# First modulation by halves of the channels, with the first four projection units begun on the first half

## Chip, core and metric

The kernel runs on one core of one Trainium2 chip. The metric is the device time of one execution in microseconds, lower is better. The time before is the median of three runs, 2643.65 us (2641.43 to 2645.2).

## What is computed

One layer of a hybrid diffusion backbone over 1024 latent tokens and 256 context tokens of 1024 channels. What bears on the change is its beginning:

```python
mod = (jax.nn.silu(c) @ w_mod[l] + b_mod[l])[:, None, :]
sh1, sc1, g1, sh2, sc2, g2 = jnp.split(mod, 6, axis=-1)
modc = (jax.nn.silu(c_ctx) @ w_mod[l] + b_mod[l])[None, None, :]
...
xn = modulate(rms_norm(x), sh1, sc1)
cn = modulate(rms_norm(h_ctx), csh1, csc1)
yg, xr, q, k, v, gr, gn = split_in(xn @ w_in[l] + b_in[l])
```

Behind it come the recurrent branch, neighbourhood attention, the merge and a mixture of 16 experts, which the change leaves alone.

## The kernel before

All weights come as chunks of 128 x 2048 floats (1 MB) and are split into a high and a low part of a rounded type: ScalarE writes the high part (a cast), VectorE the low part (a subtraction). A product is then three matmuls (`mm3`, L187 to L189). The text calls the 24 matmuls of 8 channel blocks, 128 output columns and 512 tokens a unit, and the three of one channel block a step.

Every engine and every DMA queue works through its instructions in the order in which the program writes them. That order is written out by hand, so an instruction that waits holds up all that the program put behind it on its engine.

The stage `stage_qkv` begins with the modulation. The shift and scale of the 1024 channels are 8 products of a 4-row vector with chunks `wm` 0 to 7: chunks 0 to 3 give the shifts, 4 to 7 the scales, and chunks 0, 1, 4, 5 belong to the first 512 channels (channel blocks k = 0 to 3), 2, 3, 6, 7 to the others (k = 4 to 7). Before, they are worked through in the order 0 to 7, chunks 0, 1, 2 and 7 as plain floats (L440), 3 to 6 split (`split_wm`, L409 and L410) and multiplied in two parts (L438). `columns(h)` turns the rows of half h into columns and adds the bias (`modc`). The sync queue brings chunks 0 and 1, the first four token tiles, chunks 2 to 7, projection chunks 0 and 1, the other four token tiles, and then the tables cos and sin.

A group is four token tiles (the last has the two context tiles). `hat(g, junk)` normalizes it: a square with a running sum on ScalarE (L360), the reciprocal root in small steps, a scaling on VectorE (L364). `turn(g, k, tag)` transposes channel block k on TensorE into a PSUM buffer (L372; there are two buffers of the tag "pt" and four of "pq"). `fill(g, k)` applies the modulation on ScalarE (`xraw`, L381, three buffers) and splits the result, `xh` on GpSimd (L391) and `xl` on VectorE (L392). `later(g)` is a generator: step k turns block k and fills block k - 1.

`rotary` computes two units (one x 0, one x 1), takes each out of PSUM on ScalarE (L543, L546), rotates the pair with two multiplications on GpSimd and four operations on VectorE (L554 to L559), and splits the two results with `out_parts`, a cast on ScalarE (L479) and a subtraction on VectorE (L481) each. For the first group of heads the order is q for tokens 0 to 511, in whose first unit `rest` does the turns and fills of k = 6 and 7, then hat(1), the split of projection chunk 1 and hat(2); k for tokens 0 to 511 with `later(1)` from its eighth step on (SKIP1 = 7); q for 512 to 1023 (the text calls it q1); k for 512 to 1023 with `later(2)` from its eighth step on (SKIP2 = 7); k for the context; then v.

## Time and profile before

| | |
|---|---|
| median of the runs | 2643.65 us |
| the profiled execution's own time | 2642.32 us |
| its span in the trace | 2640.5 us |
| mean granted TensorE clock, share of full | 0.975 |
| TensorE busy | 2489.4 us, 94% of the span |
| VectorE busy | 1913.5 us, 72% |
| ScalarE busy | 1486.2 us, 56% |
| DMA, mean over the span | 251 GB/s |

The profiled execution ran 1.3 us under the median; 1.8 us of its time lie outside the span. Times in rows of the trace count from the start of the span. Busy time of TensorE is that of pipelined matmuls, so a busy engine isn't an engine at its peak.

### The profile page before, as it was taken

The numbers are of one execution on the slowest core, as the hardware profiler recorded it, in microseconds if no ns is written. First come the engines' busy times: TensorE is split into PE (matmuls) and PEld (weight loads), VectorE is DVE, ScalarE is ACT, GpSimd is POOL, SyncE is SP. The second block draws the span as 40 slices with busy tenths as digits, with TensorE's granted clock in tenths as the row PEclk, the third lists the DMA queues.
The fourth block names the chain that finished last, engine by engine and source line by source line (L and its number), as shares of the span: only waits on it lengthen the run. The fifth ranks groups of instructions, "written<-read, shape, count | busy, mean of one in ns | idle before, by whom it ended". The sixth has DMA issues, their size and how long they took to land.

```text
span 2640.5 us, 34427 instructions
## 1 busy us (share of the span) xinstructions
PE 2489.4 (94%) x13401; PEld 2034.4 (77%) x13401; DVE 1913.5 (72%) x2294; ACT 1486.2 (56%) x1567; POOL 376.3 (14%) x328
## 2 busy tenths in 40 slices
PE   7999999999998899999987499999999999999996
PEld 4887888777887777777976388888888888888885
DVE  5675633655564667675477789888898988898888
ACT  5321125456655555564333277777777777777776
POOL 1321110222221000000254200000000000000001
PEclk9999999999999899999998699999999999999998
DMA  8454441122214979656865599999999999999985
GB/s 273 143 197 170 173 142 50 50 86 90 72 66 146 317 213 283 199 150 217 284 200 200 195 361 374 370 381 378 373 372 380 373 373 372 372 369 377 373 304 223
DMA packets 258386, 662.84 MB, mean 251 GB/s; under 512 B 18032, under 2 KB 35584, under 8 KB 248496
## 3 DMA queue, kind: packets, MB, share of 16 engines
q1 hardware_dynamic: 233040, 577.84, 61.7%
q0 software_dynamic: 17952, 71.65, 8.0%
q10 hardware_dynamic: 7232, 11.16, 1.4%
q8 instruction: 105, 1.72, 0.3%
q14 instruction: 57, 0.47, 0.1%
HBM read 586.07 MB, written 74.53 MB: 250 GB/s over the span
## 4 chain that ended last, share of the span: by engine, by line
PE 74%; DVE 10%; ACT 6%; issue 5%; DMA 4%; POOL 1%; SPq 0%; ACTq 0%; POOLq 0%; DVEq 0%
PE pm L187 9%; PE pm L188 9%; PE pm L189 9%; PE po L187 4%; PE po L188 4%; PE po L189 4%; PE pv L954 3%; PE pt L932 3%; PE pq L187 2%; PE pq L188 2%; PE pq L189 2%; PE sp L905 2%; PE mm L187 2%; PE mm L189 2%; PE mm L188 2%
## 5 line engine op out<-in xcount | busy, mean ns | idle before, releaser
L98 DVE TENSOR_TENSOR w1l<-ring,w1h 128x2048 fp32r<-128x2048 f32 x150 | 343.5, 2290 | 74.8 <-ACT w1h L181 74.3
L181 ACT CAST w1h<-ring 128x2048 fp32r<-128x2048 f32 x150 | 286.5, 1910 | 87.2 <-PE pm L189 41.0
L98 DVE TENSOR_TENSOR x0l<-ring,x0h 128x2048 fp32r<-128x2048 f32 x105 | 241.5, 2300 | 49.3 <-ACT x0h L181 47.9
L98 DVE TENSOR_TENSOR w0l<-ring,w0h 128x2048 fp32r<-128x2048 f32 x97 | 223.6, 2305 | 73.7 <-ACT w0h L181 73.5
L181 ACT CAST w0h<-ring 128x2048 fp32r<-128x2048 f32 (+1 forms) x100 | 189.1, 1892 | 91.9 <-DMA ring<-wqkv 40.3
L181 ACT CAST x0h<-ring 128x2048 fp32r<-128x2048 f32 x106 | 202.4, 1909 | 54.8 <-PE pm L189 33.1
L1762 POOL DMA_INDIRECT d_acc<-y,idx x15 | 50.6, 3373 | 850.4 <-DVE y L1761 850.4
L187 PE MATMUL pm<-w0h,xeh 128*128 128x512 f32 x384 | 154.7, 403 | 0.0
L909 DVE CUSTOM_DVE_ANT_0 e<-sp,bias 128x640 f32<-128x640 f32 (+1 forms) x128 | 100.9, 788 | 71.5 <-PE sp L905 54.8
L188 PE MATMUL pm<-w0l,xeh 128*128 128x512 f32 x384 | 152.7, 398 | 0.0
L189 PE MATMUL pm<-w0h,xel 128*128 128x512 f32 x384 | 152.6, 397 | 0.0
L934 ACT COPY et<-pt 128x640 f32<-128x640 f32 (+1 forms) x128 | 85.3, 666 | 110.0 <-PE pt L932 109.2
L187 PE MATMUL pm<-x0h,xeh 128*128 128x512 f32 x320 | 128.4, 401 | 0.0
L187 PE MATMUL pm<-w1h,xeh 128*128 128x512 f32 x320 | 127.7, 399 | 0.0
L188 PE MATMUL pm<-x0l,xeh 128*128 128x512 f32 x320 | 126.7, 396 | 0.4 <-DVE x0l L98 0.4
L189 PE MATMUL pm<-w1h,xel 128*128 128x512 f32 x320 | 126.8, 396 | 0.0
L188 PE MATMUL pm<-w1l,xeh 128*128 128x512 f32 x320 | 126.7, 396 | 0.0
L189 PE MATMUL pm<-x0h,xel 128*128 128x512 f32 x320 | 126.2, 394 | 0.0
L187 PE MATMUL pp<-xh,w1h 128*128 128x512 f32 (+1 forms) x304 | 116.8, 384 | 9.3 <-ACT xr L701 4.8
L917 ACT ACTIVATE e<-e,mx 128x640 f32<-128x640 f32 (+1 forms) x128 | 103.2, 806 | 32.4 <-DVE mx L911 32.0
L188 PE MATMUL pp<-xl,w1h 128*128 128x512 f32 (+1 forms) x304 | 116.2, 382 | 0.0
L189 PE MATMUL pp<-xh,w1l 128*128 128x512 f32 (+1 forms) x304 | 116.1, 382 | 0.0
(461 smaller groups left out, 6946.9 us busy)
## 6 DMA issues: line engine op xcount, KB each, us to landing
ring<-w_exp_down SPq DMA_DIRECT2D x104, 1024.0 KB
ring<-w_exp_gate SPq DMA_DIRECT2D x101, 1024.0 KB
ring<-w_exp_up SPq DMA_DIRECT2D x100, 1024.0 KB
k<-d_k SPq DMA_DIRECT2D x64, 320.0 KB
wmr<-wm POOLq DMA_DIRECT2D x16, 1024.0 KB, 8.7
ring<-wrnn SPq DMA_DIRECT2D x16, 1024.0 KB
ring<-wqkv SPq DMA_DIRECT2D x12, 1024.0 KB
bias<-bias SPq DMA_DIRECT2D x16, 704.0 KB
```

Source lines behind the costliest of these rows:

```text
L98: (engine or self.lo_engine).tensor_sub(lo, x, hi)
L181: self.nc.scalar.copy(hi, x)
L187: mm(out, wh, xh, start=first, stop=False)
L188: mm(out, wh, xl, start=False, stop=False)
L189: mm(out, wl, xh, start=False, stop=last)
L905: nc.tensor.matmul(sp[:, a:a + m], q[:, s * 128:(s + 1) * 128], ks[part][:, k0:k0 + m], start=part == 0, stop=part == 1)
L909: nc.vector.tensor_tensor_reduce(e[:, :w], sp[:, c0:c0 + w], b[:, b0:b0 + w], 1.0, -3.0e38, op0=ALU.add, op1=ALU.max, accum_out=mx[:, 0:1])
L917: nc.scalar.activation(e[:, :w], e[:, :w], AF.Exp, bias=mx[:, 1:2], accum_out=mx[:, 2:3])
L932: nc.tensor.transpose(pt[:, c * 128:(c + 1) * 128], e[:, c * 128:(c + 1) * 128], self.ident)
L934: nc.scalar.copy(et[:, :w], pt[:, :w])
L954: nc.tensor.matmul(pv[j * 64:(j + 1) * 64, (s % 4) * 128:(s % 4 + 1) * 128], v[:, t, j * 64:(j + 1) * 64], state[n - 1 + j][:, c * 128:(c ...
L1762: nc.gpsimd.indirect_dma_start(out=self.d_acc[:, :], out_offset=bass.IndirectOffsetOnAxis(ap=self.idx[:, e:e + 1], axis=0), in_=y[:, :], i ...
```

## The change

The loads are put in another order: the four token tiles first, then modulation chunks 0, 1, 4 and 5, projection chunk 0, and then 2, 3, projection chunk 1, 6 and 7 (5 and 2 into buffers that later hold the parts of projection chunk 1). The modulation is computed in the order 0, 1, 4, 5 (first half) and 2, 3, 6, 7; now chunks 0 and 1 alone are plain and six are split, into the part of `xh` and `xl` that later tokens will fill. With the first half known, k = 0 to 3 of the first 512 tokens are filled, and the four units of q and k for these tokens run their steps k = 0 to 3 (`products`), among them the products of the second half. Then they do k = 4, 5 and k = 6, 7. hat(1) stands behind the fill of k = 7 and the steps of k = 5; later(1) begins in the second unit's step k = 6 and ends in q1; hat(2) stands behind q1. `rotary` is cut into `evict` and `turned`, which do what they did.

```diff
-    def load(self, engine=None):
-        while self.nload < len(self.chunks) and self.free:
+    def load(self, engine=None, most=9):
+        most += self.nload
+        while self.nload < min(len(self.chunks), most) and self.free:
...
+        self.xn, self.c_xn = self.open_("xn", side="right", bufs=1)
+        self.xh = self.xn.tile([128, KC, NT], F32R, name="xh")
+        self.xl = self.xn.tile([128, KC, NT], F32R, name="xl")
...
-        def load_wm(i):
-            t = wp.tile([128, 2048], F32, name="wm", tag="wm", bufs=4)
+        def load_wm(i, tag=None):
+
+            t = wp.tile([128, 2048], F32, name="wm", tag="wm", bufs=3) if tag is None else \
+                self.hip.tile([128, 2048], F32R, name=tag, tag=tag).bitcast(F32)
             nc.sync.dma_start(t, I["wm"][i])
-            wm.append(t)
-
+            wm[i] = t
+
+
+        for t in range(4):
+            load_x(t, nc.sync)
         load_wm(0)
         load_wm(1)
-        for t in range(4):
-            load_x(t, nc.sync)
-        load_wm(2)
-        load_wm(3)
+        load_wm(4)
+        load_wm(5, "w1h")
+        S.load(most=1)
+        load_wm(2, "w1l")
...
-        def hat(g, junk):
+        def hat(g):
             t0, n = groups[g]
             ss = st.tile([128, 4], F32, name="ss", tag="ss", bufs=2)
+            junk = st.tile([128, 512], F32, name="xraw", tag="xraw", bufs=3).bitcast(BF16)
             for i in range(n):
-                nc.scalar.activation(junk, x_t[t0 + i].rearrange("p (a b) -> p a b", a=junk.shape[1]), AF.Square,
-                                     accum_out=ss[:, i:i + 1])
+                nc.scalar.activation(junk, x_t[t0 + i], AF.Square, accum_out=ss[:, i:i + 1])
...
-        def split_wm(i):
-            wh = wp.tile([128, 2048], F32R, name="wmh", tag="wmh", bufs=2)
-            wl = wp.tile([128, 2048], F32R, name="wml", tag="wml", bufs=2)
-            nc.scalar.copy(wh, wm[i])
-            nc.vector.tensor_sub(wl, wm[i], wh)
+        def split_wm(i, n):
+
+            ts = slice(512 + n * 256, 768 + n * 256)
+            wh, wl = self.xh[:, :, ts], self.xl[:, :, ts]
+            x = wm[i].rearrange("p (k n) -> p k n", k=8)
+            nc.scalar.copy(wh, x)
+            nc.vector.tensor_sub(wl, x, wh)
             parts[i] = (wh, wl)
...
+        pcs = {}
+
+        def modulate(i, copy):
+
+            pm = ps.tile([4, 256], F32, name="pt", tag="pt", bufs=2)
+            for k in range(8):
+                if i in parts:
+                    for n, part in enumerate(parts[i]):
+                        nc.tensor.matmul(pm, sr[:, k], part[:, k], start=k + n == 0, stop=k + n == 8)
+                else:
+                    nc.tensor.matmul(pm, sr[:, k].bitcast(F32), wm[i][:, k * 256:(k + 1) * 256],
+                                     start=k == 0, stop=k == 7)
+            copy(rows[:, i * 256:(i + 1) * 256], pm)
+
+        def columns(i):
+
+            a, h = i // 4, i % 4 // 2
+            if h not in pcs:
+                pcs[h] = ps.tile([128, 4, 2, 4], F32, name="pv", tag="pv", bufs=2)
+            for x in range(2):
+                nc.tensor.transpose(pcs[h][:, 2 * (i % 2) + x, a],
+                                    rows[:, (2 * i + x) * 128:(2 * i + x + 1) * 128], self.ident[:4, :4])
+
+        def modulation(h):
+
+            pc = pcs[h]
...
-        hat(0, wp.tile([128, 2, 512], F32, name="junk"))
-        for i in range(8):
-            if i == 3:
-                for k in range(4):
-                    turn(0, k, "pq")
-            pm = ps.tile([4, 256], F32, name="pt", tag=("pt", "pv")[i % 2], bufs=2)
-            for k in range(8):
-                ks = slice(k * 256, (k + 1) * 256)
-                if i in parts:
-                    for n, part in enumerate(parts[i]):
-                        nc.tensor.matmul(pm, sr[:, k], part[:, ks], start=k + n == 0, stop=k + n == 8)
-                else:
-                    nc.tensor.matmul(pm, sr[:, k].bitcast(F32), wm[i][:, ks], start=k == 0, stop=k == 7)
-            if i == 6:
-                columns(0)
-                S.split(1, pieces=2)
-            if i < 4:
-                load_wm(i + 4)
-                if i > 1:
-                    split_wm(i + 1)
-            if i == 3:
-                S.load()
-            if i in (3, 4):
-                split_wm(i + 2)
-            (nc.scalar.copy if i in (0, 1, 2, 5, 6) else nc.vector.tensor_copy)(rows[:, i * 256:(i + 1) * 256], pm)
-            if i == 6:
-                for k in range(3):
-                    shifted(0, k)
+        hat(0)
+        modulate(0, nc.scalar.copy)
+        modulate(1, nc.scalar.copy)
+        load_wm(3)
+        S.load(most=1)
+        for k in range(4):
+            turn(0, k, "pq")
+        split_wm(4, 0)
+        split_wm(5, 1)
+        modulate(4, nc.scalar.copy)
+        load_wm(6)
+        for i in (0, 1):
+            columns(i)
+        S.split(1, pieces=2)
+        modulate(5, nc.scalar.copy)
+        load_wm(7)
         for t in range(4, 8):
             load_x(t, nc.sync)
-        columns(1)
+        for i in (4, 5):
+            columns(i)
+        modulation(0)
+        for k in range(4):
+            fill(0, k)
+        q = S.take8(most=0)
+        units = [ps.tile([128, 512], F32, name="pq", tag="pq", bufs=4) for x in range(2)]
+
+        def products(x, w, ks):
+
+            hi, lo = w
+            cs = slice((x % 2) * 128, (x % 2 + 1) * 128)
+            for k in ks:
+                self.mm3(units[x], hi[:, k, cs], lo[:, k, cs], self.xh[:, k, :512], self.xl[:, k, :512], k == 0, k == 7)
+
+        split_wm(2, 2)
+        split_wm(3, 0)
+        for k in range(4):
+            for x in range(2):
+                products(x, q, (k,))
+        S.split(1, pieces=2)
+        modulate(2, nc.vector.tensor_copy)
+        split_wm(6, 1)
+        modulate(3, nc.vector.tensor_copy)
+        split_wm(7, 2)
+        for i in (2, 3):
+            columns(i)
+        kw = S.take8(hold=True, most=0)
+        units += [ps.tile([128, 512], F32, name="pq", tag="pq", bufs=4) for x in range(2)]
+        products(2, kw, range(4))
+        modulate(6, nc.scalar.copy)
+        products(3, kw, range(2))
+        modulate(7, nc.scalar.copy)
+        for i in (6, 7):
+            columns(i)
+        modulation(1)
...
         for k in (4, 5):
             turn(0, k, "pt")
-        for k in range(6):
+        products(3, kw, range(2, 4))
+        for k in (4, 5):
             fill(0, k)
-        for t in range(8, 10):
-            load_x(t, nc.gpsimd)
...
+        def evict(which, g, x, pm, n):
+            r = p.tile([128, 512], F32, name="qr", tag=f"qr{x}", bufs=2)
+            if which == "q":
+                nc.scalar.activation(r[:, :n], pm[:, :n], AF.Identity, scale=0.125,
+                                     bias=bq8[:, 2 * g + x:2 * g + x + 1])
+            else:
+                nc.scalar.activation(r[:, :n], pm[:, :n], AF.Identity, bias=self.pk("bk", 2 * g + x))
+            return r
+
+        def turned(which, g, a, b, tok, n):
...
+        def rotary(which, g, hi, lo, tok, n, steps=(None, None)):
+            ab = []
+            for x in range(2):
+                pm = ps.tile([128, 512], F32, name="pq", tag="pq", bufs=4)
+                self.unit(pm[:, :n], hi, lo, x * 128, tok, n, steps[x])
+                ab.append(evict(which, g, x, pm, n))
+                beside()
+            turned(which, g, *ab, tok, n)
...
+        for k in (4, 5):
+            products(0, q, (k,))
+            products(1, q, (k,))
+            turn(0, k + 2, "pt")
+            products(2, kw, (k,))
+            products(3, kw, (k,))
+            fill(0, k + 2)
+        for t in range(8, 10):
+            load_x(t, nc.gpsimd)
+        hat(1)
+        more = later(1)
+        for x, w in ((0, q), (1, q), (2, kw), (3, kw)):
+            for k in (6, 7):
+                products(x, w, (k,))
+                if x > 0:
+                    next(more, None)
+            units[x] = evict("qk"[x // 2], 0, x % 2, units[x], 512)
+            if x % 2:
+                turned("qk"[x // 2], 0, units[x - 1], units[x], 0, 512)
         for g in range(4):
-            hi, lo = S.take8(most=0 if g == 0 else 9)
             if g == 0:
-                def rest():
-                    for k in (6, 7):
-                        turn(0, k, "pq")
-                        fill(0, k)
-                        yield
-
-                    hat(1, self.xl[:, 0:2, 512:1024])
-                    S.split(1)
-                    yield
-                    hat(2, self.xl[:, 0:4, 1024:1280])
-                    yield
-
-                more = rest()
-                q = hi, lo
-                rotary("q", 0, *q, 0, 512, (lambda: next(more, None), None), ("pv", "pq"))
-                hi, lo = S.take8(hold=True)
-                rotary("k", 0, hi, lo, 0, 512, (late(later(1), SKIP1),) * 2)
-                rotary("q", 0, *q, 512, 512)
+                hi, lo = kw
+                rotary("q", 0, *q, 512, 512, (lambda: next(more, None),) * 2)
+                hat(2)
```

## Rows read from the trace of the kernel before

**Rows 1.** The page: its span and the busy time of the engines.

```profile
span 2640.5 us, 34427 instructions
...
PE 2489.4 (94%) x13401; PEld 2034.4 (77%) x13401; DVE 1913.5 (72%) x2294; ACT 1486.2 (56%) x1567; POOL 376.3 (14%) x328
```

**Rows 2.** Busy time by windows: window, length, engines, granted clock, DMA share, GB/s.

```profile
9.00:17.00 8.00, 8.00 (x31) 2.88 (x29) 0.00 (x0) 2.80 (x5) 0.00 (x0) 1.00 1.04 241
18.00:36.00 18.00, 11.84 (x82) 6.89 (x83) 13.22 (x16) 11.38 (x12) 0.00 (x0) 1.00 1.01 420
43.70:66.21 22.51, 19.08 (x82) 14.07 (x81) 18.78 (x29) 13.84 (x22) 9.88 (x11) 1.00 0.47 162
66.21:108.27 42.06, 39.49 (x217) 32.56 (x216) 30.79 (x39) 20.13 (x31) 22.19 (x25) 1.00 0.29 100
```

**Rows 3.** TensorE's timeline to 109 us: start, duration, line, operation, idle before.

```profile
8.24 9.14 PE L440 MATMUL pt<-wm,sr 128*4 128x256 f32 x32 [8.24 <-DVE sr L352]
20.60 3.62 PE L440 MATMUL pt<-wm,sr 128*4 128x256 f32 x16 [3.22 <-DMA wm<-wm]
...
33.46 0.28 PE L438 MATMUL pt<-wml,sr 128*4 128x256 f32 x1 [1.62 <-DVE wml L410]
...
35.08 0.28 PE L438 MATMUL pt<-wml,sr 128*4 128x256 f32 x1
...
43.70 0.50 PE L187 MATMUL pv<-xh,w0h 128*128 128x512 f32 x1
...
66.21 0.60 PE L372 MATMUL pt<-ident,xin 128*128 128x128 f32 x4
...
108.27 0.28 PE L187 MATMUL pv<-w0h,xh 128*128 128x256 f32 x1
```

**Rows 4.** ScalarE's timeline to 110 us.

```profile
23.06 1.91 ACT L409 CAST wmh<-wm 128x2048 fp32r<-128x2048 f32 x1 [1.75 <-DMA wm<-wm]
24.88 0.35 ACT L452 COPY rows<-pt 4x256 f32<-4x256 f32 x1
...
36.46 2.00 ACT L181 CAST w0h<-ring 128x1024 fp32r<-128x1024 f32 x2 [0.70 <-DMA ring<-wqkv]
...
39.11 2.11 ACT L381 ACTIVATE xraw<-pq,modc 128x512 f32<-128x512 f32 x3 [0.40 <-DVE modc L426]
...
49.80 1.05 ACT L360 ACTIVATE xl<-xin 128x1024 fp32r<-128x1024 f32 x1
...
77.46 0.69 ACT L546 ACTIVATE qr<-pq,par 128x512 f32<-128x512 f32 x1
83.56 0.62 ACT L479 CAST ohi<-t 128x512 fp32r<-128x512 f32 x1 [5.40 <-DVE t L558]
```

**Rows 5.** VectorE's timeline to 110 us.

```profile
25.00 2.29 DVE L410 TENSOR_TENSOR wml<-wm,wmh 128x2048 fp32r<-128x2048 f32 x1 [0.43 <-ACT wmh L409]
...
38.99 2.36 DVE L115 TENSOR_TENSOR w0l<-ring,w0h 128x1024 fp32r<-128x1024 f32 x2
...
43.68 3.75 DVE L392 TENSOR_TENSOR xl<-xraw,xh 128x512 fp32r<-128x512 f32 x4
...
55.97 2.74 DVE L364 TENSOR_SCALAR xin<-xin,rs_y 128x1024 f32<-128x1024 f32 x4
...
71.05 0.69 DVE L392 TENSOR_TENSOR xl<-xraw,xh 128x512 fp32r<-128x512 f32 x1 [1.27 <-POOL xh L391]
...
80.41 1.78 DVE L554 TENSOR_TENSOR t<-qr,cos 128x512 f32<-128x512 f32 x1
```

**Rows 6.** GpSimd's timeline to 110 us.

```profile
70.40 2.40 POOL L391 TENSOR_SCALAR xh<-xraw 128x512 fp32r<-128x512 f32 x3 [4.47 <-ACT xraw L381]
```

**Rows 7.** Windows: an idle stretch of TensorE, and the stretches after two such.

```profile
207.36:212.25 4.89, 0.01 (x1) 0.01 (x1) 4.78 (x8) 0.00 (x0) 0.00 (x0) 0.81 0.27 101
212.25:217.30 5.05, 5.05 (x24) 5.05 (x24) 2.97 (x6) 0.00 (x0) 0.54 (x1) 0.50 1.02 298
...
486.98:490.30 3.32, 3.32 (x8) 2.64 (x9) 0.31 (x1) 3.32 (x7) 3.03 (x3) 0.50 0.52 217
```

More of the change, by code (lines that the diff above doesn't have):

```diff
@@ L414, in stage_qkv @@
         bm = self.par[:, _cols["bsh1"][0]:_cols["bsc1"][1]].rearrange("p (a k) -> p k a", a=2)
-        def columns(h):
-            pc = ps.tile([128, 4, 2, 4], F32, name="pv", tag="pv", bufs=2)
-            for k in range(4):
-                for a in range(2):
-                    j = 8 * a + 4 * h + k
-                    nc.tensor.transpose(pc[:, k, a], rows[:, j * 128:(j + 1) * 128], self.ident[:4, :4])
+        pcs = {}
[18 more added lines that the diff above has]
+            pc = pcs[h]
             m = modc[:, 4 * h:4 * h + 4]
@@ L534, in beside @@
                 next(s, None)
-        def rotary(which, g, hi, lo, tok, n, steps=(None, None), tags=("pq", "pq")):
-            ab = []
-            for x in range(2):
-                pm = ps.tile([128, 512], F32, name=tags[x], tag=tags[x], bufs=4 if tags[x] == "pq" else 2)
-                self.unit(pm[:, :n], hi, lo, x * 128, tok, n, steps[x])
-                r = p.tile([128, 512], F32, name="qr", tag=f"qr{x}", bufs=2)
-                if which == "q":
-                    nc.scalar.activation(r[:, :n], pm[:, :n], AF.Identity, scale=0.125,
-                                         bias=bq8[:, 2 * g + x:2 * g + x + 1])
-                else:
-                    nc.scalar.activation(r[:, :n], pm[:, :n], AF.Identity, bias=self.pk("bk", 2 * g + x))
-                ab.append(r)
-                beside()
-            a, b = ab
+        def evict(which, g, x, pm, n):
[7 more added lines that the diff above has]
+        def turned(which, g, a, b, tok, n):
             if tok < SEQ:
@@ L601, in stage_qkv @@
             else:
+                hi, lo = S.take8()
                 for tok in (0, 512):
```

6 lines of the change are left out of this document (1 added, 5 removed).

## The prediction

> **What bounds the kernel now.** The page comes first: TensorE is busy 94% of a span of 2640.5 us [rows 1], so a gain must be work or idle time taken from it. The change touches only the start, so I went to windows of the first 110 us and to the engines' timelines there. The loads come in a closed row: four token tiles at 241 GB/s, chunks at 420 [rows 2]. A token tile of 0.52 MB so takes 2.2 us, a chunk of 1.05 MB 2.5. The first projection product starts at 43.70, the turns for the second group at 66.21, and the first group of heads is through q and k at 108.27, where v begins [rows 3]. From 43.70 to 66.21 TensorE idles 22.51 - 19.08 = 3.4 us, from 66.21 to 108.27 another 42.06 - 39.49 = 2.6 [rows 2]. So after 43.70 there are 6.0 us of idle time to win, plus what an earlier start gives. What follows 108.27 is the same program before and after, and TensorE leads it; I carry every shift at 108.27 to the end.
>
> **First half.** I work out the new order as a list of times, each engine in its program order, with the durations of the rows. In the old run the products of chunk 0 start at 8.24, when the vector is ready. Now four token tiles stand ahead of chunk 0, 4 x 2.2 = 8.7 us, and it lands at about 15.7 (old landing about 7.0: the first bytes move near 2.8, one chunk takes 2.5 and the receipt, estimated from the later ones, 1.7). The first two plain products took 9.14 us together, the next one alone 3.62 [rows 3]: the engine's first microseconds are slow. I take 9.1 again, so chunks 0 and 1 are through at 24.9. ScalarE can cast chunk 4, landed at 20.7, only behind the copy of row 1: 0.35 + 1.91 [rows 4] to 27.2. VectorE's subtraction, 2.29 [rows 5], ends at 29.5. Split products run 33.46 to 35.36 once their low part is there, 1.9 us [rows 3]: to 31.3. ScalarE copies the row (0.35) and casts projection chunk 0 behind it, 2.0, to 33.7; VectorE's second piece (1.2 of 2.36) ends at 35.1, three small operations of the modulation at 35.7. The fill takes 0.8 on ScalarE (2.11 for three, overlapped) and 0.8 on GpSimd: first product at 37.4, 6.3 us before the old 43.70.
>
> **Second half.** Four pieces of xl take 3.75 [rows 5], to 41.2; the 24 matmuls, 5.6 us at 0.2335 each (the pitch of 24 steps in the old units), end at 43.8, and split chunks 2 and 3 at 47.7. Here VectorE is late. Behind the fills it has subtractions for 2 and 3 (4.6), projection chunk 1 (2.4), the copy of row 2 (0.4), the subtraction for 6 (2.3) and only then the copy of row 3: 51.3. The columns of row 3 wait for it, TensorE idles 3.5 us, and all its next products queue behind them. From 51.6: 12 matmuls 2.8, chunk 6 1.95, 6 matmuls 1.4, chunk 7 1.95, columns and copies 0.7, two turns 0.9, 6 matmuls 1.4: 62.7. The second half's modulation is ready at 61.0, although its last chunk has landed near 38: it is bound by engine order, not by loads. After 0.8 us for the first fill of k = 4, steps k = 4 and 5 of four units with two turns take 6.5, and three steps more 2.1: with small waits TensorE has done 27 of the 32 steps at 72.4. The old kernel had done 24 at 66.21 and had 39.5 us of work left to 108.27 [rows 2]; three steps less (2.1) leave the new one 37.4 us.
>
> **Four new waits.** First, hat(1). ScalarE reaches its squares behind the fill of k = 7, at 69.4 (turn 7 on TensorE to 68.6, 0.8 for the fill). In the old run the squares began at 49.80 and the scalings ended at 55.97 + 2.74 = 58.71 [rows 4, 5], 8.9 us, under 24 steps of q and k. In the new one the turns need all four tiles at 69.4 + 9.1 = 78.5, while TensorE has work to 72.4: 6.1 us idle. Second and third, the rotations. Behind an eviction the ScalarE queue holds the casts of the rotated pair, and behind those the fills of later(1). In the old run the eviction at 77.46 was followed by the first cast at 83.56 [rows 4]; of that wait 3.15 us lie behind the multiplication's start at 80.41 [rows 5]. The old program has seven steps between rotation and turns; the new one has none, and with two "pt" buffers TensorE stops after two turns. That costs 4.8 us behind q's rotation and 5.4 behind k's. Fourth, hat(2): before, its chain ended long before its turns. Now it waits behind q1's rotation; its squares, root and two scalings take 5.3, and it starts when k's first unit, which covers the rotation, is nearly through: 5.3 us idle. Sum: 6.1 + 4.8 + 5.4 + 5.3 = 21.6.
>
> So v begins at 72.4 + 37.4 + 21.6 = 131.4 instead of 108.27: **+23.1 us**.
>
> **The clock.** After an idle stretch of 4.89 us the granted clock is 0.50, that is 1.2 GHz, for the next 5.05 us; after another of about that length for 3.32 [rows 7]. Five other idle stretches of 3.4 to 7.1 us are followed by it too. A new wait so costs up to 2.5 us more, half of 5.05. Behind the first the slow steps partly fill the second wait (+0.5 together, and the second is then under 3 us); the third and the fourth cost 2.5 each. I take +5.5, bounds 0 and 9: together **+28.6 us**. On the profiled execution, 2642.32, that is 2670.9; on the median, 1.3 higher, 2672.
>
> **GpSimd beside VectorE.** In the rows four subtractions xl take 0.94 us each beside GpSimd's passes, and one at 71.05 takes 0.69 in the middle of a run of three passes of 0.8 [rows 5, 6]; I use 0.94. The Trainium skill, GPSIMD Engine Reference, Specifications, says that GpSimd shares its SBUF interfaces with VectorE and contends with instructions of two SBUF inputs, which these are. If each waited out a pass, a pair would take 0.8 + 0.69 = 1.5 and my list would give +30 instead of +28.6; the row at 71.05 shows that it needn't.
>
> **Terms that no row shows.** The casts of modulation chunks into strided rows of `xh` and the squares into a half-width scratch: between the contiguous row's price (1.91, 1.05) and twice that for the six casts, of which two are on the path, +4; I take the row's, since size and engine are the same. The products' slow first microseconds: 1.9 us if they come again, 0 if not; I take 1.9. The multiplication at 80.41 (1.78) ran beside GpSimd; at the 0.69 of a subtraction of that shape the two rotation waits shrink by 1 each. All low bounds together (clock 0, no slow start, shorter rotations) give 28.6 - 5.5 - 1.9 - 2 = +19, all high ones 28.6 + 3.5 + 4 = +36.
>
> **Rivals.** (a) The waits come, but the clock holds: +23, 2667, where the new waits are broken up by more than I see. For it: a wait of 1.6 us at 33.46 [rows 3] left no trace in the granted clock of 18 to 36 [rows 2]. (b) Everything is covered and it is faster: the start at 37.4 stands, and TensorE never idles again to the end of the stretch. It then has 19.1 + 39.5 us of old work and 8.6 more (four split products of 1.95 and the columns, which now lie behind the first unit): 37.4 + 67.2 = 104.6, or -3.7; with no slow first products -5.6, 2638. It decides where hat(1) ends before 72.4; for that ScalarE would have to reach its squares 6 us before the fill that its queue puts ahead of them. (c) No measurable change: the list's waits are half as long and only two of the four appear, 2643 to 2649. Against both: the same durations, run through the old order, give the old kernel's v at 108.0, against 108.27. (d) The change doesn't make the first products earlier, if the loads of chunks 4 and 5 wait: the first eight loads wait for nothing, so this is part of the upper end, +34, 2678.
>
> **How the numbers follow.** Chances: forecast (about +28, 2663 to 2679) 0.55; (a) and shorter waits, +11 to +23, 0.22; (d) and dearer terms 0.08; (c) 0.09; (b) 0.06. 0.2% of this time is 5.3 us, about what a measurement can tell. So faster 0.05, same 0.10, slower 0.85. The range reaches down into (a), to 2655, and up to 2681; what is left out is (b), (c) and the ends.
>
> **What would show it.** In the profile after: the first product near 37; `modc` of the second half near 61, behind VectorE's queue and not behind a load; TensorE idle for 6 us before the first turn of the second group, with VectorE's `xin` as releaser; two idle stretches of 3 to 5 us released by ScalarE's `xraw`; one of 5 before the context's turns, released by `xin`; granted clock 0.5 behind the longest of them; v near 131 to 137; and no difference in the stages behind. The prediction is wrong if ScalarE's squares run before the fill of k = 7, if the turns don't wait, or if a stage behind takes the shift up.

## The result and the profile after

The changed kernel takes **2669.30 us** (median of 4 runs, 2667.51 to 2669.65) against 2642.54 (4 runs, 2639.01 to 2645.20) on the same chip: ratio **1.0099, interval 1.0085 to 1.0112**. It is 26.8 us slower; forecast were 2672 us and +28.6. The profiled execution took 2667.51 us, 1.8 us under the median; its rows, like those of every run below, are those of one execution.

The page after, span and busy time of the engines, answers to [rows 1]:

```profile
span 2665.6 us, 34437 instructions
...
PE 2498.1 (94%) x13401; PEld 2041.6 (77%) x13401; DVE 1912.2 (72%) x2296; ACT 1490.3 (56%) x1571; POOL 375.6 (14%) x328
```

The number of TensorE instructions is the same (13401 both times), but TensorE is busy 8.7 us longer with it, and the span is 25.1 us longer. Both have to be found in the first 137 us. TensorE's timeline after (start, duration, line, operation, idle before with its releaser), against [rows 3]:

```profile
14.85 9.84 PE L437 MATMUL pt<-wm,sr 128*4 128x256 f32 x32 [14.85 <-DMA wm<-wm]
...
37.89 0.80 PE L188 MATMUL pq<-xh,w0h 128*128 128x512 f32 x1 [2.20 <-POOL xh L400]
...
51.77 0.28 PE L447 MATMUL pv<-ident,rows 4*128 4x4 f32 x2 [1.00 <-DVE rows L439]
...
77.08 1.04 PE L381 MATMUL pt<-ident,xin 128*128 128x128 f32 x2 [4.36 <-DVE xin L373]
...
87.70 0.55 PE L381 MATMUL pt<-ident,xin 128*128 128x128 f32 x3 [4.06 <-ACT xraw L390]
...
98.63 0.59 PE L381 MATMUL pt<-ident,xin 128*128 128x128 f32 x3 [4.56 <-ACT xraw L390]
...
120.69 0.45 PE L381 MATMUL pt<-ident,xin 128*128 128x128 f32 x1 [4.46 <-DVE xin L373]
...
136.54 0.28 PE L188 MATMUL pv<-w0h,xh 128*128 128x256 f32 x1
```

The first product of a projection stands at 37.89 instead of 43.70: the early start that the change makes is there. But v begins at 136.54 instead of 108.27. Between lie four waits of 4.06 to 4.56 us in front of turns, 17.44 us together, two released by VectorE's scaled tiles (`xin`) and two by a copy of ScalarE (`xraw`). Their reasons stand in the queues of these two engines. (The second group, token tiles 4 to 7, is called strips 4 to 7 in some of the expectations below.) ScalarE after, against [rows 4]:

```profile
25.00 1.89 ACT L420 CAST xh<-wm 128x2048 fp32r<-128x2048 f32 x1
...
69.03 0.78 ACT L390 ACTIVATE xraw<-pt,modc 128x512 f32<-128x512 f32 x1 [2.40 <-PE pt L381]
69.71 1.04 ACT L370 ACTIVATE xraw<-xin 128x1024 bf16<-128x1024 f32 x1
...
85.75 0.62 ACT L528 CAST ohi<-t 128x512 fp32r<-128x512 f32 x1 [4.29 <-DVE t L604]
86.35 0.62 ACT L528 CAST ohi<-qr 128x512 fp32r<-128x512 f32 x1
86.87 1.44 ACT L390 ACTIVATE xraw<-pt,modc 128x512 f32<-128x512 f32 x2
...
96.67 0.62 ACT L528 CAST ohi<-t 128x512 fp32r<-128x512 f32 x1 [4.61 <-DVE t L604]
97.27 0.62 ACT L528 CAST ohi<-qr 128x512 fp32r<-128x512 f32 x1
97.80 1.44 ACT L390 ACTIVATE xraw<-pt,modc 128x512 f32<-128x512 f32 x2
...
115.42 0.63 ACT L528 CAST ohi<-qr 128x512 fp32r<-128x512 f32 x1 [1.31 <-DVE qr L605]
115.95 1.05 ACT L370 ACTIVATE xraw<-xin 128x1024 bf16<-128x1024 f32 x1
```

VectorE after, against [rows 5]:

```profile
51.30 0.41 DVE L439 COPY rows<-pt 4x256 f32<-4x256 f32 x1
...
60.93 0.17 DVE L454 TENSOR_TENSOR modc<-pv,par 128x16 f32<-128x16 f32 x1 [7.02 <-PE pv L447]
...
76.17 2.74 DVE L373 TENSOR_SCALAR xin<-xin,rs_y 128x1024 f32<-128x1024 f32 x4 [0.34 <-DVE rs_y L298]
```

The squares of token tiles 4 to 7 begin at 69.71, behind the fill at 69.03 (in the kernel before at 49.80, [rows 4]). The fills at 86.87, for which TensorE stands still until 87.70, are queued on ScalarE behind a cast that waits 4.29 us for VectorE's rotation; those at 97.80, in front of the turn at 98.63, stand behind the casts of the next rotation in the same way. And the squares of the context begin at 115.95, behind the casts of q1's rotation.

The rest of TensorE's loss is clock. Busy time by windows after (window, length, busy time of PE, PEld, DVE, ACT, POOL with the number of instructions, granted clock, DMA share, GB/s), for the stretches between the waits, against the last two of [rows 2]:

```profile
37.89:50.77 12.88, 12.88 (x58) 9.36 (x58) 12.06 (x10) 10.56 (x8) 2.75 (x3) 0.75 0.90 236
51.76:72.72 20.96, 20.48 (x111) 15.21 (x111) 5.52 (x9) 6.57 (x11) 4.29 (x6) 1.00 0.22 74
77.08:83.64 6.56, 6.06 (x21) 4.07 (x21) 4.38 (x6) 1.46 (x2) 2.64 (x3) 0.63 0.00 1
87.70:94.07 6.37, 6.37 (x28) 5.04 (x28) 4.16 (x5) 3.32 (x5) 5.74 (x6) 0.73 0.25 74
98.63:116.23 17.60, 17.60 (x70) 13.91 (x70) 5.90 (x9) 4.19 (x7) 5.46 (x5) 0.90 0.20 68
120.69:136.54 15.85, 15.72 (x88) 13.37 (x89) 10.68 (x14) 6.22 (x12) 8.63 (x13) 0.82 0.12 46
```

A clock of 0.75 over 12.88 us means that a quarter of that time, 3.2 us, was lost if TensorE had work throughout. So summed, the six rows give 3.2 + 0 + 2.4 + 1.7 + 1.8 + 2.9 = 12.0 us. This is a little too much: at 0.50 one product follows the other after 0.43 us, at 1.00 after 0.2335, so a slow stretch costs 45% of its length and not half, and the sum is nearer to 10.9. In the kernel before, the clock of these stretches was 1.00 [rows 2].

**The balance** up to v, from these rows and [rows 2, 3]. Before: 43.70 plus 64.57 us, of which TensorE is busy 58.56. After: 37.89 plus 98.65, of which it is busy 79.12. That makes -5.8 for the start, +20.6 of busy time and +13.5 of idle time, +28.3. Of the busy time 10.9 to 12.0 is clock, 7.4 the 64 split products of chunks 2, 3, 6 and 7 at 0.116 us each, which used to lie ahead of the first projection; the rest, 1.2 to 2.3, fits the transposes of their rows and the turns of k = 4 and 5, which lay there too. So without the slow clock and with no more idle time than before, v would still come some 3 to 4 us later: the products that were moved cost more than the 5.8 us of the start. Behind v the changed kernel is 3.2 us shorter in these two executions (2529.1 us against 2532.3): a wait at 207.36 us of 4.89 us before [rows 7] is 3.61 us in it, with 3.1 us of slow clock behind it for 5.05. So 25.1 us of span are left of 28.3; by the medians it is 26.8.

### The profile page after: what moved, and what is told of

The parts are those of the page before. It is cut to its first block, busy times and chain, and to the rows that moved or that the text cites. A ratio compares the mean times of both kernels' runs of the same rounds, so it can differ in the third digit from the quotient of the medians.

```text
span 2665.6 us, 34437 instructions
## 1 busy us (share of the span) xinstructions
PE 2498.1 (94%) x13401; PEld 2041.6 (77%) x13401; DVE 1912.2 (72%) x2296; ACT 1490.3 (56%) x1571; POOL 375.6 (14%) x328
## 4 chain that ended last, share of the span: by engine, by line
PE 75%; DVE 10%; issue 6%; ACT 5%; DMA 3%; POOL 1%; SPq 0%; ACTq 0%; POOLq 0%; DVEq 0%
PE pm L188 9%; PE pm L189 9%; PE pm L190 9%; PE po L188 4%; PE po L190 4%; PE po L189 4%; PE pv L1014 3%; PE pt L992 3%; PE pp L188 2%; PE pp L189 2%; PE pp L190 2%; PE pq L188 2%; PE pq L189 2%; PE sp L965 2%; PE pq L190 2%
## 5 line engine op out<-in xcount | busy, mean ns | idle before, releaser
L182 ACT CAST w1h<-ring 128x2048 fp32r<-128x2048 f32 (+1 forms) x151 | 286.6, 1898 | 84.6 <-PE pm L190 41.0
```

The source lines that it names most:

```text
L182: self.nc.scalar.copy(hi, x)
```

## The experiments

Each run also has its v, the start of the v projection, and the rest of its span behind v, both from its one profiled execution. The ratios are to the kernel before, run beside it on the same chip; the runs were made on several chips. One execution is not the median: the profiled ones lie up to 4.7 us from it (e8_group1_and_casts), and the 32 plain products at the start, which no run edits, took 8.37 to 9.87 us in these traces. A difference of about 1 us in v, or of a few us in the rest, says nothing by itself. The waits are numbered as in the prediction: 1 hat(1), 2 and 3 the rotations, 4 hat(2).

| run | time, us | ratio, interval | v | rest |
|---|---|---|---|---|
| before | 2642.54 | 1 | 108.27 | 2532.3 |
| changed kernel | 2669.30 | 1.0099 (1.0085 to 1.0112) | 136.54 | 2529.1 |
| e1_hat1_early | 2666.28 | 1.0097 (1.0080 to 1.0114) | 131.4 | 2532.5 |
| e2_rot_late | 2669.53 | 1.0108 (1.0091 to 1.0125) | 135.4 | 2531.6 |
| e3_hat2_early | 2662.97 | 1.0087 (1.0070 to 1.0104) | 130.3 | 2529.1 |
| e6_fillers | 2668.62 | 1.0107 (1.0090 to 1.0124) | 134.9 | 2531.6 |
| e13_both_hats | 2658.10 | 1.0060 (1.0043 to 1.0076) | 126.1 | 2533.4 |
| e5_early_casts | 2664.83 | 1.0086 (1.0069 to 1.0102) | 132.8 | 2530.7 |
| e7_group1_first | 2655.64 | 1.0051 (1.0034 to 1.0068) | 122.6 | 2530.4 |
| e8_group1_and_casts | 2652.27 | 1.0042 (1.0025 to 1.0059) | 117.9 | 2527.7 |
| e9_all_moved | 2650.40 | 1.0042 (1.0028 to 1.0055) | 112.3 | 2534.0 |
| e10_no_early_products | 2675.49 | 1.0133 (1.0118 to 1.0149) | 140.8 | 2532.7 |
| e11_clock_early | 2648.61 | 1.0022 (1.0013 to 1.0031) | 110.4 | 2540.4 |
| e12_clock_and_context | 2649.66 | 1.0030 (1.0021 to 1.0040) | 108.1 | 2541.5 |

**Wait 1 alone.** The squares and scalings of token tiles 4 to 7 are issued ahead of the second half's products and fills:

```diff
         split_wm(7, 2)
+        hat(1)
 ...
-        hat(1)
         more = later(1)
```

> The changed kernel with hat(1) put behind the split of modulation chunk 7, where ScalarE is idle from 50.6 to 56.9 us and the second group's tiles have landed. Theory (four waits made by the order of the queues): the idle stretch of 4.4 us before the first turn of the second group goes, the waits at the two rotations and before the context's turns stay, v begins some 5 us earlier, 2664 us. Rival (ScalarE and VectorE are simply late and the wait comes back at the next turn): the sum of the idle stretches between 66 and 137 us stays 17.4 us, 2669 us.

The squares began at 48.86 instead of 69.71, v came 5.1 us earlier and wait 1 was gone. The median is 3 us lower, though the intervals of the two ratios overlap; in the profiled executions the wait behind v went from 3.61 back to 5.21 us. The gain at v is about the wait (4.36) and the 2.4 us of clock behind it, less 1.65 us by which the next wait grew (4.06 to 5.71).

**Waits 2 and 3 alone.** Both rotations are issued behind the last fill of token tiles 4 to 7:

```diff
             units[x] = evict("qk"[x // 2], 0, x % 2, units[x], 512)
-            if x % 2:
-                turned("qk"[x // 2], 0, units[x - 1], units[x], 0, 512)
+        def rest():
+            yield from more
+            for x in (0, 2):
+                turned("qk"[x // 2], 0, units[x], units[x + 1], 0, 512)
+                yield
```

> The changed kernel with the two rotations of q and k for the first 512 tokens put behind the last fill of the second group (steps 4 and 5 of q1), nothing else moved. Theory: the two waits of 4.1 and 4.6 us released by ScalarE's fill go, since no cast of a rotated pair stands ahead of a fill; the rotations now pile up ahead of hat(2), so the wait before the context's turns grows from 4.5 to about 7; sum about -8, 2661 us. Rival (the fills themselves are what is slow, 0.8 us on each of three engines): TensorE still waits at turns 3 and 7, less than 3 us gained, 2666 us or more.

This missed. The two waits were gone, and in their place stood one of 15.93 us in front of the context's turns. ScalarE's timeline of this run shows why:

```profile
104.57 0.62 ACT L528 CAST ohi<-qr 128x512 fp32r<-128x512 f32 x1 [2.46 <-DMA d_q<-ohi]
...
111.27 0.62 ACT L528 CAST ohi<-t 128x512 fp32r<-128x512 f32 x1 [4.91 <-DVE t L604]
114.83 0.62 ACT L528 CAST ohi<-qr 128x512 fp32r<-128x512 f32 x1 [2.95 <-DMA d_k<-ohi]
115.36 1.05 ACT L370 ACTIVATE xraw<-xin 128x1024 bf16<-128x1024 f32 x1
```

Three rotations now follow each other. `ohi` and `olo` have three buffers each, so the later casts wait for a store to land; the squares of the context, 115.36, wait behind it on ScalarE. I had not counted the stores. Rotations can be moved, but not brought together.

**Wait 4 alone.** The squares and scalings of the context become a step of their own behind the last fill of token tiles 4 to 7, within q1:

```diff
+        def rest():
+            yield from more
+            hat(2)
+            yield
 ...
-                hat(2)
                 S.drop()
```

> The changed kernel with hat(2) put into q1, behind the last fill of the second group. Theory: the wait of 4.5 us before the context's turns goes, and with it the slow clock from 119.5 to 126.3; about -6, 2663 us; the three other waits stay as they are. Rival (the context's turns wait for q1's rotation, not for the normalization): the wait moves to ScalarE's fill as releaser and keeps over 3 us, 2667 us or more.

v came 6.2 us earlier, and the other three waits stayed (4.34, 3.94, 4.37 us). So this wait cost its 4.46 us and 1.8 us more, which fits the clock behind it (2.9 by the windows).

**The waits filled instead of removed.** 66 matmuls without use are put into the four waits, so that TensorE has something to run:

```diff
+        def fillers(n):
+            pm = ps.tile([128, 512], F32, name="pv", tag="pv", bufs=2)
+            for i in range(n):
+                nc.tensor.matmul(pm, q[0][:, 0, :128], self.xh[:, 0, :512], start=i == 0, stop=i == n - 1)
```

> The changed kernel with products that nobody reads put into the four waits (17, 15, 17 and 17 matmuls of 512 columns, 4.0, 3.5, 4.0 and 4.0 us at full clock), so that TensorE is not idle there. Nothing else moves. Theory (the idle stretches bring the 1.2 GHz clock, and it costs on the path): the granted clock stays 1.00 from 72 to 137 us; v begins 4 to 6 us earlier although TensorE does more, 2664 us. Rival (the slow stretches lie under other engines' work and cost nothing): the clock rises but v doesn't move, 2669 us or later.

v moved by only 1.7 us and the time by 0.7, which is near the rival and looks like a cheap clock. Counted out it isn't. From 72.9 us to v TensorE is busy 57.4 us of 61.96, of which 66 fillers at 0.235 are 15.5: 41.9 for the real work, where the changed kernel is busy 45.8 us of 63.82 from 72.72 to v. So the clock gave back 3.9 us; the fillers, standing in front of turns, cost 2.0 more than the idle time that they fill (15.5 and 4.6 of rest against 18.1). The clock fell again in two of four places (79.4 and 99.9), behind waits of 0.3 us between single turns and one of 2.16.

**Waits 1 and 4 together**, the edits of two runs above:

> Both squares-and-scalings of the later strips are given earlier at once (those of strips 4 to 7 behind the casts of the last weight chunk, those of the context behind the turns of strips 4 to 7), the rotations stay where they are. Theory (each wait is TensorE standing still for the late turn, and they are independent): the gains of the two single edits add, 5.1 + 6.2, so the v projection begins at 136.5 - 11.3 = 125.2 us and the time is some 2660 (2657 to 2664), with two waits of about 4.5 us left, those of the two rotations. Rival (VectorE and GpSimd are what limits the stretch, the waits only move on): v begins at 128 or later and the rotation waits grow by what was gained.

v at 126.1: the gains add to within 1 us. The waits of the two rotations stayed, 5.70 and 4.96 us, about as long as with the first edit alone (5.71 and 4.69). The rival, that a wait removed comes back further on, got 0.9 us of 11.4.

**The first half.** The casts of chunks 4 and 5 are issued ahead of the copies of rows 0 and 1, and ScalarE copies row 3:

```diff
+        split_wm(4, 0)
+        split_wm(5, 1)
         modulate(0, nc.scalar.copy)
         modulate(1, nc.scalar.copy)
 ...
-        modulate(3, nc.vector.tensor_copy)
+        modulate(3, nc.scalar.copy)
```

> The change as it is, but the casts of weight chunks 4 and 5 are issued ahead of the two copies of rows 0 and 1, and row 3 is copied by ScalarE instead of VectorE; the three waits behind are untouched. Theory: the first projection product waits for chunk 4's cast and subtraction, which stand behind the row copies, and TensorE's 2.05, 2.2 and 1.0 us of idle time at 27, 36 and 51 us go down to 1 to 2 us together; v begins 3 to 5 us earlier, at 131.5 to 133.5, and the time is 2664 to 2667. Rival (the casts wait for the weight chunks' DMA, not for ScalarE): the first product stays at 37.9 and v at 136.5, time 2669.

The first product came at 34.22 (37.89 in the changed kernel, 36.76 to 37.37 in the five runs above, which leave this part alone) and v 3.7 us earlier. So the start was set by the order of ScalarE's queue, not by the loads; the wait for row 3 went to 0.24 us.

**All turns of token tiles 4 to 7 ahead of the rotations.** They are made within the first two units, two per step of products:

```diff
         split_wm(7, 2)
+        hat(1)
 ...
                 products(x, w, (k,))
-                if x > 0:
+                if x < 2:
+                    next(more, None)
                     next(more, None)
 ...
+            if x == 1:
+                hat(2)
```

> The squares and scalings of strips 4 to 7 are given early as in the first experiment, and all eight turns and fills of these strips are stepped within units 0 and 1 (two per lot of products) so that they are ahead of both rotations on VectorE and GpSimd; the squares of the context stand behind unit 1's eviction. The rotations keep their distance from each other, so no store buffer piles up. Theory (the waits come from turns whose scaled strips or PSUM slots stand behind hat and rotation on VectorE and GpSimd): all four waits go, 17.4 us of TensorE's idle time with them, less some 2 us of the extra ones that the denser steps cause; v begins at 117 to 122 us and the time is 2651 to 2657, 3 to 5 thousandths above the kernel before. Rival (VectorE and GpSimd are filled to the brim here, the steps come too dense): products of units 0 and 1 wait for the fills instead, v begins at 126 or later, 2660 or more.

v at 122.6, 0.6 us above what I gave: waits 1 to 3 were gone, but one of 9.79 us stood in front of the third turn of the context.

**The edits of the two runs above together.**

> The edits of the two previous runs together. Theory: the gains add; v begins at 113 to 118, the time is 2646 to 2653, that is within 4 thousandths of the kernel before; what stays of the loss are the half-clock stretches and the smaller waits of the early part. Rival (early and later waits cover each other): not below the better of the two alone.

v at 117.9, 0.9 us below the sum of the two gains. The wait of 9.76 us stayed. TensorE's row and ScalarE's queue in front of it, in this run:

```profile
105.36 0.69 PE L381 MATMUL pt<-ident,xin 128*128 128x128 f32 x2 [9.76 <-ACT xraw L390]
```

```profile
98.32 0.62 ACT L529 CAST ohi<-t 128x512 fp32r<-128x512 f32 x1 [4.95 <-DVE t L605]
101.84 0.62 ACT L529 CAST ohi<-qr 128x512 fp32r<-128x512 f32 x1 [2.91 <-DMA d_k<-ohi]
102.37 1.89 ACT L182 CAST w0h<-ring 128x2048 fp32r<-128x2048 f32 x1
104.17 0.68 ACT L592 ACTIVATE qr<-pq,par 128x512 f32<-128x512 f32 x1
104.75 1.01 ACT L390 ACTIVATE xraw<-pt,modc 128x256 f32<-128x256 f32 x2
```

The copy that would free the PSUM buffer, 104.75, stands behind the casts of q1's rotation, the next weights and an eviction. It is the same mechanism as waits 2 and 3.

**This one removed too.** The context is turned within k's first unit, and q1's rotation is issued behind that unit:

```diff
+                ab = both("q", q, lambda: None)
+                S.drop()
+                S.load()
+                more = later(2)
+                def between():
+                    turned("q", 0, *ab, 512, 512)
+                    S.split(1)
+                kk = both("k", kw, between)
+                turned("k", 0, *kk, 512, 512)
```

> As the run with group 1 first and early casts, and in addition the context's turns and fills (nine steps) are stepped in the first unit of K's strips 4 to 7, before Q's second rotation is issued; the casts of the next weights come behind that rotation. In the run before, TensorE stood still from 95.60 to 105.36 us at the third turn of the context, whose PSUM slot waited for a ScalarE copy queued behind the casts of that rotation. Theory (every wait of the changed kernel is such a queueing behind rotations, squares or copies): the 9.76 us and the half clock behind them (at most 2.7 us of 97.9 to 108.1) go, 1 to 2.5 us of denser waits come; v begins at 107 to 111 us, as in the kernel before (108.27), and the time is 2636 to 2645, ratio 0.998 to 1.002. Rival (VectorE, ScalarE and GpSimd have too much to do in this stretch; a wait removed comes back at the next place): v at 114 or later, ratio 1.003 or more.

v at 112.3, between the two expectations: of the 9.76 us 3.16 stayed. The total came out as the rival's: v came 5.5 us earlier than in the run before, and the ratio stayed at 1.0042. The wait behind v, 2.15 us there, is 7.54 us here. That doesn't show that an early v brings the wait back. From v to the end of this wait it is 101.2 to 104.5 us in every run without this edit and in the kernel before, whose v is earlier still (104.0); here it is 108.6, and 111.2 and 111.8 in e11_clock_early and e12_clock_and_context, which keep this edit. So the longer wait goes with this edit, which among other things puts q1's rotation and its stores closer to k's; which part of it does it was not tried.

**The change without its early start.** The 42 matmuls (14 steps) that run with one half of the modulation are put behind the second half:

```diff
         split_wm(3, 0)
-        for k in range(4):
-            for x in range(2):
-                products(x, q, (k,))
         S.split(1, pieces=2)
 ...
-        products(2, kw, range(4))
         modulate(6, nc.scalar.copy)
-        products(3, kw, range(2))
 ...
         modulation(1)
+        for k in range(4):
+            for x in range(2):
+                products(x, q, (k,))
+        products(2, kw, range(4))
+        products(3, kw, range(2))
```

> The change without its early start: the 42 matmuls (14 of the 32 steps of the four units) that the changed kernel runs between 37.89 and 61 us, with one half of the modulation, stand behind the second half of the modulation; everything else is as in the changed kernel. Theory (the early start is worth what it does, the loss comes from the four waits and the moved products of the modulation): the second half of the modulation is ready some 4 us earlier (57 for 61.35 us), 14 steps of 0.70 us, 9.9 us, come after it, v begins 3 to 7 us later, at 139.5 to 143.5, and the time is 2671 to 2676. Rival (VectorE and ScalarE pace the stretch behind, so that the early products gain nothing): v within 1.5 us of 136.5 or earlier, 2669 or less.

v at 140.8, 4.3 us later, 2675.49 us. VectorE begins the second half's modulation at 55.3 instead of 60.93. So the early start does what it is meant to do, and is worth 4.3 us up to v; the four waits are there without it too (4.35, 3.93, 4.37 and 4.48 us), so they come from the new order behind it.

**The price of the clock alone.** Twelve matmuls without use fill the 2.80 us in front of the first product in the best order so far:

```diff
         for i in (4, 5):
             columns(i)
+        pm = ps.tile([128, 512], F32, name="pt", tag="pt", bufs=2)
+        for i in range(12):
+            nc.tensor.matmul(pm, self.xh[:, 0, 512:640], self.xh[:, 0, 512:1024], start=i == 0, stop=i == 11)
         modulation(0)
```

> The version with all three moves, and twelve matmuls more whose result nobody reads (128x128 by 128x512, from the cast halves of chunk 4) behind the transposes of the first half's modulation, where TensorE stood still from 31.52 to 34.32 us and the granted clock was 0.5 from 33.9 to 40.7 us. This asks for the price of the half clock alone, at one place. Theory (a half-clock stretch that falls into products costs half its length): twelve matmuls of 0.23 us fill the wait, the clock stays, the products from 34.3 to 40.7 us take half of 6.4 us, 3.2 us, less, and v begins at 108.5 to 109.5 instead of 112.3; the time is 2645 to 2648 if nothing behind takes it back. Rival (the products are paced by ScalarE's and VectorE's fills of the first four columns of x, the clock costs nothing): v within 1 us of 112.3.

Windows from the first product to the end of the same 24 matmuls, first without the fillers (and of these the slow part by itself), then with them:

```profile
34.32:43.06 8.74, 8.74 (x25) 6.54 (x25) 8.23 (x7) 8.61 (x7) 2.75 (x3) 0.64 1.03 283
34.32:40.72 6.40, 6.40 (x14) 4.76 (x15) 5.89 (x6) 6.26 (x6) 2.75 (x3) 0.50 1.03 305
```

```profile
33.57:39.97 6.40, 6.17 (x25) 4.44 (x25) 5.89 (x6) 6.26 (x6) 2.75 (x3) 1.00 1.02 319
```

Without the fillers the granted clock is 0.50, which is 1.2 GHz, for the first 6.40 us; with them it holds at 1.00, and the 24 matmuls take 2.34 us less. That is less than the 3.2 us of the theory, in part because the second product now waits 0.23 us for a fill. The next wait that both runs have, in front of the context's turns, begins at 88.39 instead of 91.44, 3.05 us earlier, but 0.75 of these are not the clock's: this execution was ahead by as much before the fillers (its last transposes of rows stand at 30.48 instead of 31.23), since its first 32 products began 0.23 us sooner and took 9.02 us instead of 9.55. Of the 3.05 us 1.9 arrive at v (110.4 for 112.3), so v misses the theory's 108.5 to 109.5; after that wait the clock is now slow for twice as long (90.6 to 97.4).

**The last wait thinned.** The context's turns begin three steps of products later, two per step then:

```diff
+                    def step():
+                        calls.append(1)
+                        for _ in range(2 if len(calls) > 3 else 0):
+                            next(more, None)
```

> As the run before, and the context's turns begin three lots of products later in their unit, two per lot then, because the first of them waited 3.16 us (91.44 to 94.60) for a ScalarE copy behind the casts of a rotation, with half clock from 95.3 to 98.7 us behind it. Theory (waits): 1.5 to 3 us of that wait and up to 1.7 us of clock go, v begins at 105 to 108, ahead of the kernel before (108.27), and the time is 2638 to 2645. Rival (it is the same three engines' work, denser steps wait for GpSimd instead): v as in the run before. A second rival for the total: the wait behind v, at 207 us in the kernel before (4.89 us) and at 213 us in the version with all three moves (7.54 us), grows by what was gained, and the time stays near 2650 whatever v does.

v at 108.1, where the kernel before has it (108.27), and none of the change's waits in front is longer than 1.78 us. Yet the time stays at 2649.66, 1.0030 of the kernel before, as the second rival has it. First the view of waits of this run for TensorE between 105 and 225 us (tile and line that wait, what they wait for, us in total, times, longest), then VectorE's timeline up to 219.84, where the longer of the two waits ended:

```profile
PE pv L188 <- DVE vo L708: 11.2, 2, 8.4
```

```profile
206.67 0.42 DVE L534 TENSOR_TENSOR olo<-qr,ohi 128x256 fp32r<-128x256 f32 x1 [0.51 <-DMA d_k<-olo]
214.14 0.42 DVE L534 TENSOR_TENSOR olo<-qr,ohi 128x256 fp32r<-128x256 f32 x1 [7.04 <-DMA d_k<-olo]
214.48 2.28 DVE L99 TENSOR_TENSOR w0l<-ring,w0h 128x2048 fp32r<-128x2048 f32 x1
216.68 0.68 DVE L708 TENSOR_TENSOR vo<-pv,bv 128x512 f32<-128x512 f32 x1
...
219.10 0.68 DVE L708 TENSOR_TENSOR vo<-pv,bv 128x512 f32<-128x512 f32 x1
```

VectorE waits 7.04 us for an `olo` buffer whose store has not landed, and the evictions of v's PSUM buffers (`vo`) are queued behind it. The kernel before has the same wait at 207.36, for 4.89 us [rows 7]. Here there are 11.2 us in two places, 6.3 us more. And TensorE works 8.9 us at half clock behind them (from 133.6 to 136.8 and from 219.8 to 225.6) for 5.05 in the kernel before, which costs some 2 us more. Together that is most of the 9.2 us by which the rest of the span is longer (2541.5 against 2532.3).

Part of why the stores are slow can be read off the DMA queues. q1 carries the stores, q0 the 1 MB chunks `wmr` that GpSimd loads; packets, MB, share of 16 engines. The kernel before from 204.5 to 208.5 and from 200 to 204 us, then this run from 209 to 214:

```profile
q1 hardware_dynamic: 193, 0.38, 24.5%
```

```profile
q0 software_dynamic: 97, 0.70, 46.0%
q1 hardware_dynamic: 87, 0.17, 10.9%
```

```profile
q0 software_dynamic: 129, 0.93, 44.9%
q1 hardware_dynamic: 132, 0.26, 13.5%
```

Nearly alone the stores move 95 GB/s (0.38 MB in 4 us), so one of 0.26 MB takes 2.8 us, an estimate; beside a chunk they move 43 and 52 GB/s, and in this run a chunk falls into the wait of 7.04 us. Whether other places for these loads, or more buffers of `ohi` and `olo`, would end the wait was not tried. No version that I ran beats the kernel before.

## Why the prediction was right, point by point

- **The sign and the size** came out: +28.6 predicted at v, +28.27 measured; 2672 predicted, 2669.30 measured. Of the 2.7 us between, 1.1 is the time before (2643.65 then, 2642.54 with a fourth run), 0.3 the shift at v, and the most of the rest the assumption that every shift at 108.27 is carried to the end: of 28.3 us at v, 26.8 reach the medians.
- **First half**: first product at 37.4, measured 37.89. The slow first products were there (9.84 us for 32, taken 9.1). The casts into strided rows, which no row of the kernel before could show, cost the contiguous row's price, as taken (1.89 at 25.00 for 1.91), and so did the squares (1.04 at 69.71 for 1.05).
- **Second half**: modulation ready at 61.0, measured at 61.5 (three operations from 60.93 on); it is bound by the order of VectorE's queue, as said, row 3 being copied at 51.30. That TensorE idles 3.5 us there was mis-sized: 1.00, since the 24 products before it ended at 46.73, 2.9 us later than in my list, most of them at half clock. 27 of 32 steps were done at 72.72, predicted 72.4: the shorter idle stretch paid for the slow clock.
- **The four waits** are where they were put, with the releasers named, and the runs that removed waits 1 and 4 gave back about what each cost in the trace, clock included. Waits 2 and 3 went in both orders tried, but with the rotations brought together a longer one came in their place. Their sum was mis-sized: 17.44 us for 21.6. The largest part is wait 1, 4.36 for 6.1: the turns need the tiles one after the other, so TensorE begins when the first is scaled (77.08) and not when all four are (76.17 + 2.74 = 78.91).
- **The clock** was mis-sized the other way: 12.0 us by the windows for the 5.5 taken, above the upper bound of 9. Behind the four waits alone it is 8.8, within the bound; 3.2 more fall on the first products, behind the wait of 2.20 us, and for these the prediction had no term. Without the clock my remaining work of 37.4 us from 72.4 on is right: 45.8 of busy time measured, less 8.8 of clock, is 37.0.
- So the waits, taken 4.2 us too long, and the idle stretch of the second half, 2.5 too long, cancelled a clock taken 6.5 too short. The forecast was right by its mechanism (start, moved products, four waits), but its closeness is largely luck. Rival (a), that the clock holds, and (b), that everything is covered, are out; (d) too, since the first product is early. (c), half the waits, was reached only by reordering. One of the prediction's own signs of being wrong, a stage behind that takes the shift up, is there in small: 1.5 us by the medians, 3.2 in the profiled pair.
- GpSimd beside VectorE was read wrongly from the rows. In the changed kernel the pairs of pass and subtraction come every 1.20 us in one run of fills (subtractions at 88.38, 89.59, 90.79 and 91.99), between the 0.94 taken and the 1.5 of the alternative. Each subtraction there takes 0.69, but the pass that starts within one takes 1.00, and a pass alone 0.62:

```profile
90.79 0.69 DVE L401 TENSOR_TENSOR xl<-xraw,xh 128x512 fp32r<-128x512 f32 x1 [0.51 <-POOL xh L400]
90.95 1.00 POOL L400 TENSOR_SCALAR xh<-xraw 128x512 fp32r<-128x512 f32 x1 [0.20 <-ACT xraw L390]
...
66.72 0.62 POOL L400 TENSOR_SCALAR xh<-xraw 128x512 fp32r<-128x512 f32 x1 [2.40 <-ACT xraw L390]
```

  So a subtraction of 0.69, such as the one at 71.05 on which the prediction rests here, is no sign that the two engines don't hinder each other. The Trainium skill, GPSIMD Engine Reference, Specifications, says that GpSimd shares its SBUF interfaces with VectorE and contends with instructions of two SBUF inputs; these rows agree with it.

## What to carry to other kernels

An earlier start is worth only what the work behind it can use. Before a stage is moved forward, list what stood hidden under it (here squares, scalings and rotations under 24 steps of products) and where each stands in its engine's queue afterwards; the four waits so found were removed here by issuing the small work earlier, not by speeding anything up, though each new order brought another wait elsewhere. Keep operations that need store buffers apart from each other, and read the first waits behind the changed stage too: they can take a gain back, as a queue of stores did here.

## What the runs showed of the hardware

- Slow clock came behind waits of 2.05 to 2.81 us at the start of this kernel (0.50 from 33.9 to 40.7 us behind a wait of 2.80), and in five of six runs behind one of 1.66 to 1.70 in front of the columns of row 3; behind the sixth, 1.65 us, the clock stayed at 1.00. In the kernel before a wait of 3.22 us at 20.60 [rows 3] left it at 1.00 [rows 2]. So the length of a wait alone didn't tell here whether the clock falls.
- At half clock a product comes every 0.43 us instead of every 0.23. Holding the clock through one stretch of 6.4 us gave back 2.3 us.
- The same 32 products at the start of the kernel took 8.37 to 9.87 us from execution to execution, without any edit.
- VectorE's product of the rotation takes 1.77 us beside GpSimd's product and 0.69 without it. The first two rows are from the changed kernel, the third from e8_group1_and_casts, where GpSimd's last product ends at 79.86:

```profile
81.53 1.35 POOL L601 TENSOR_TENSOR t<-qr,sin 128x512 f32<-128x512 f32 x1 [0.51 <-ACT qr L588]
81.67 1.77 DVE L600 TENSOR_TENSOR t<-qr,cos 128x512 f32<-128x512 f32 x1
```

```profile
82.53 0.69 DVE L601 TENSOR_TENSOR t<-qr,cos 128x512 f32<-128x512 f32 x1
```

  The Trainium skill, GPSIMD Engine Reference, Specifications, says that instructions of VectorE with two inputs in SBUF contend with GpSimd; these rows agree with it.
- The stores of rotated pairs are slow enough to set the pace: with three buffers to turn over, casts and subtractions of the rows above waited up to 7.04 us for one to land.
